# Closing MLP weights in units of two row tiles by 512 columns

## The chip, the cores and the metric

The kernel runs on one core of a Trainium2 chip. The metric is the device time of one execution in microseconds, the median of several runs. TensorE is PE in the rows, its weight loads are PEld, VectorE is DVE, ScalarE is ACT, GpSimd is POOL and SyncE is SP, which issues the transfers.

## What is computed

A trunk of four layers over 640 tokens (128 context, 512 latent) of width 1024. Each layer has a mixer (differential attention, neighbourhood attention, grouped-query attention, Hyena) and a squared-ReLU MLP, each with modulation, a gate and a layer norm:

```
for i in range(DEPTH):                                   # 4 layers
    mod_p = split(silu_ctx @ ada_w[i] + ada_b[i], 6)     # mod_s likewise, from c
    hp, hs = modulate(xp, mod_p[0], mod_p[1]), modulate(xs, mod_s[0], mod_s[1])
    op, os_ = mixer_i(hp, hs)
    xp = layer_norm(DN_ALPHA * xp + mod_p[2] * op, ...)  # xs likewise
    fp = relu(modulate(xp, mod_p[3], mod_p[4]) @ mlp_w1[i]) ** 2 @ mlp_w2[i]   # 1024 -> 4096 -> 1024
    xp = layer_norm(DN_ALPHA * xp + mod_p[5] * fp, ...)  # xs likewise
```

## The kernel before

All 640 tokens go through the weights together, as five tiles of 128 (`NT`). Values are fp32; for a matmul each operand is split into a rounded part and a rest, and `mm3` (lines 471 to 475) issues three matmuls: weights high with data high, weights high with data low, weights low with data high. Each matmul has its own weight load.

Weights come in units of 128 by 1024 fp32 (512 KB) in a fixed order that `weight_order` lists. `wget` (line 461) hands out a unit, starts transfers three ahead and splits units two ahead: a cast on ACT (line 450) and a difference on DVE (line 451, `hl`).

The MLP (`mlp`, line 865) runs in eight chunks of four row tiles of the hidden width. For chunk `ch` it first makes four opening units (`w1_unit`: 48 matmuls of 320 columns into a pair of banks, then Relu, Square and a split into `ff[ch]`), then it closes chunk `ch - 1` with four closing units (`w2`). A closing unit is four row tiles by 256 output columns. `quarter` (line 809) makes one group of 12 matmuls of 256 columns for each token tile, in which the `ff` tiles are the stationary operand and the weights move, and `residual` (line 647) evacuates it: a product with the gate on DVE (line 653, `gtmp`, three buffers) and an add into the residual `r` (line 660), three of four on POOL in layers 0 to 2 and all on DVE in layer 3. Chunk 7 is closed in `sublayer_end`, by `quarter` too.

Between the units, `side` (line 1530) does work of later layers, one slot behind each opening and each closing unit: a step of the next layer's modulation (`ada_step`, line 528: four multiply-adds on DVE of 128x512; at the last of eight steps, which falls behind a chunk's last closing unit, a sum over partitions by four matmuls with ones, and a copy), and, before the Hyena layer, filters (`hy_taps`, layer 0: two matmuls of 512 columns and the product `win`, line 1576; `tap_step` every third closing group) and their transforms (`hy_dft`, `hy_dft_ctx`, layers 1 and 2).

PSUM has eight banks: `b1` and `f1`, two single banks each, which `any1` (line 336) hands out in turn, and `b2` (line 340), a ring of two places of two banks each. Before the change the opening units and the filters take `b2`; closing groups, modulation sums (`ada`, `adat`) and the context transform (`hsc`) take `any1`.

The order of POOL's instructions is that of the program; those of PE, DVE and ACT are put in order when the kernel is built, by a planner with modelled durations, from the program's order as priority.

Of the kernel before, what the change touches and what calls it, by code (L numbers as in the profile page):

```python
# [18 lines left out]
P = 128  # L19
# [5 lines left out]
NT = TOK // P  # L25
# [4 lines left out]
DEPTH = 4  # L30
# [26 lines left out]
TSTEP = 3  # L57
# [138 lines left out]
def unit_b(w, k0, c0):  # L196
    return w[k0 * P:(k0 + 4) * P, c0:c0 + 256].reshape(4, P, 256).transpose(1, 0, 2).reshape(P, 1024)


def prepare(inp):  # L200
    g = {n: np.asarray(a) for n, a in inp.items()}
    o = lat_order()
    d = dict(shape_constants())
    x = np.concatenate([g["x_prompt"][0], g["x_sample"][0][o]], 0)
    d["x_tok"] = x.reshape(NT, P, D).transpose(1, 0, 2)
    d["x_t"] = x.T.reshape(KD, P, TOK).transpose(1, 0, 2)
    d["cvec"] = np.stack([g["c_ctx"], g["c"][0]], -1).reshape(KD, P, 2).transpose(1, 0, 2)
    d["ada_w"] = g["ada_w"]
    d["ada_b"] = g["ada_b"]
    d["ada_s"] = g["ada_w"][:, :, :2 * D].reshape(DEPTH, KD, P, 2, KD, P)[0].transpose(3, 1, 0, 2, 4).reshape(KD, P, 2 * D)  # L210
    d["ada_bt"] = g["ada_b"].reshape(DEPTH, 6, KD, P)[:, MODS].transpose(3, 0, 1, 2)
    d["ln_t"] = np.stack([g["ln_g"], g["ln_b"]], 2).reshape(DEPTH, 2, 2, KD, P).transpose(4, 0, 1, 2, 3)
    d["ln_g"] = g["ln_g"]
    d["ln_b"] = g["ln_b"]
    d["w1"] = np.stack([np.stack([unit_a(g["mlp_w1"][l], np.arange(f * P, f * P + P)) for f in range(32)]) for l in range(DEPTH)])
    d["w2"] = np.stack([np.stack([unit_b(g["mlp_w2"][l], 4 * ch, q * 256) for ch in range(8) for q in range(4)]) for l in range(DEPTH)])
    for nm, wq, cf in (("da", g["da_w_qkv"][0], da_cols), ("na", g["na_w_qkv"][0], na_cols)):
        d[nm + "_qk"] = np.stack([unit_a(wq, s * D + cf(j)) for j in range(8) for s in range(2)])
        d[nm + "_v"] = np.stack([unit_b(wq, 4 * kh, 2 * D + 256 * gr) for gr in range(4) for kh in range(2)])
    wq = g["gq_w_qkv"][0]  # L220
    d["gq_qk"] = np.stack([unit_a(wq, D + pair_cols(128 * i, 128 * i + 64)) for i in range(2)] + [unit_a(wq, gq_cols(j)) for j in range(8)])
    d["gq_v"] = np.stack([unit_b(wq, 4 * kh, 1280) for kh in range(2)])
    d["hy_in"] = np.stack([unit_a(g["hy_w_in"][0], np.arange(P) + p * D + (2 * gr + ct) * P) for gr, p in hy_parts() for ct in range(2)])
    rows = np.concatenate([np.arange(h * 64, h * 64 + 64) for j in range(8) for h in gq_heads(j)])
    for nm, wo in (("da", g["da_w_o"][0]), ("na", g["na_w_o"][0]), ("gq", g["gq_w_o"][0][rows]), ("hy", g["hy_w_o"][0])):
        d[nm + "_o"] = np.stack([unit_b(wo, 4 * kh, q * 256) for kh in range(2) for q in range(4)])
    ck = g["cache_da_k"][0, 0].reshape(P, D)
    d["da_ck"] = np.stack([ck[:, da_cols(j)].T for j in range(8)])
    ck = g["cache_na_k"][0, 0].reshape(P, D)
    d["na_ck"] = np.stack([ck[:, na_cols(j)].T for j in range(8)])  # L230
    ck = g["cache_gq_k"][0, 0].reshape(P, 256)
    d["gq_ck"] = np.stack([ck[:, pair_cols(128 * i, 128 * i + 64)].T for i in range(2)])
    for nm in ("da", "na", "gq"):
        d[nm + "_cv"] = g[f"cache_{nm}_v"].reshape(P, -1)
    d["da_lam"] = g["da_lambda"].reshape(1, 256)
    d["da_sub"] = g["da_subln_g"].reshape(P, 1)
    kc = np.arange(3 * P) // ROWS - 16
    rk = np.arange(3 * P) % ROWS
    qc, rq = np.arange(P) // ROWS, np.arange(P) % ROWS
    rr = rk[None, :] - rq[:, None] + 7  # L240
    cc = np.clip(kc[None, :] - qc[:, None], -15, 15) + 15
    d["na_bias"] = g["na_rel_bias"][0][:, rr, cc]
    both = pair_cols(0, 64) % 64
    part = both.reshape(2, 2, 32)[:, ::-1].reshape(-1)
    d["gq_g"] = np.stack([g["gq_q_norm"][0][both], g["gq_q_norm"][0][part], g["gq_k_norm"][0][both], g["gq_k_norm"][0][part]], 1)
    d["hy_sw"] = np.concatenate([g["hy_short_w"][0], g["hy_short_b"]], 0).reshape(4, 3, KD, P).transpose(3, 1, 2, 0)
    d["hy_w1"] = g["hy_ffn_w1"][0]
    d["hy_w2"] = g["hy_ffn_w2"][0]
    d["hy_b"] = np.stack([g["hy_ffn_b1"][0], g["hy_ffn_b2"][0], g["hy_ffn_freq"][0]], 1)
    w3 = g["hy_ffn_w3"][0].reshape(64, 2, 2, 4, 256).transpose(1, 3, 0, 2, 4).reshape(2, 4, 64, 512)  # L250
    ld = g["hy_log_decay"].reshape(2, 2, 4, 256).transpose(0, 2, 1, 3).reshape(2, 4, 1, 512)
    d["hy_w3"] = np.concatenate([np.concatenate([w3, w3], 2), np.broadcast_to(ld, (2, 4, P, 512))], 3)
    d["hy_fb"] = g["hy_filter_bias"][0]
    return {n: np.ascontiguousarray(a) for n, a in d.items()}
# [24 lines left out]
class Trunk:  # L279
# [248 lines left out]
    def ada_step(self, raw, l, m, k):  # L528

        nc = self.nc  # L530
        if k == 0:
            self.tn += 1
            self.acc = self.scr.tile([P, 2, D], F32, tag="ada", bufs=1, name=f"ada{self.tn}")
        acc = self.acc
        for h in range(2):
            for s in range(2):
                x, y = self.sil[:, k, s:s + 1], acc[:, s, h * 512:(h + 1) * 512]
                if k == 0:
                    nc.scalar.activation(y, raw[h], AF.Copy, scale=x)
                else:  # L540
                    nc.vector.scalar_tensor_tensor(out=y, in0=raw[h], scalar=x, in1=y, op0=ALU.mult, op1=ALU.add)  # L541
        if k < KD - 1:
            return
        ps = self.any1([P, 512], "ada")
        for g in range(4):
            nc.tensor.matmul(ps[32 * g:32 * g + 32], self.ones, acc[:, g // 2, g % 2 * 512:g % 2 * 512 + 512], start=True, stop=True)
        row = self.S(F32, "adarow", 512)
        if m in MODS:
            nc.scalar.copy(row, ps)
            pt = self.any1([P, 4, P], "adat")  # L550
            for j in range(4):
                nc.tensor.transpose(pt[:, j], row[:, j * P:(j + 1) * P], self.ident)
            mod = self.modt[l % 2][:, MODS.index(m)].rearrange("p (h j) s -> p h j s", j=4)
            bias = self.adab[:, l, MODS.index(m)].rearrange("p (h j) -> p h j", j=4)
            for s in range(2):
                src = pt[:, :, 64 * s:64 * s + 64:32].rearrange("p j h -> p h j")
                nc.vector.tensor_add(mod[:, :, :, s], src, bias)
            return
        bias = self.S(F32, "adabias", 512)
        nc.gpsimd.memset(bias, 0.0)  # L560
        for g in range(4):
            c = m * D + g % 2 * 512
            nc.sync.dma_start(bias[32 * g:32 * g + 1], self.a["ada_b"][l:l + 1, c:c + 512])
        nc.vector.tensor_add(row, ps, bias)
        for g in range(4):
            c = g % 2 * 512
            nc.sync.dma_start(self.gate_d[l, GATES.index(m), g // 2:g // 2 + 1, c:c + 512], row[32 * g:32 * g + 1])
# [297 lines left out]
    def mlp(self, l, nxt, last):  # L865
        nc = self.nc
        self.share = QL if last else QM
        ff = {}
        groups = 0
# [21 lines left out]
        def w1_first():  # L891
# [15 lines left out]
                        evac([ff[0][:, n, 2 * pair:2 * pair + 2, c0:c1] for n in range(2)], ps[:, :, :c1 - c0])  # L907
            self.settle()

        for ch in range(8):  # L910
            ff[ch] = self.L(F32R, f"ff{ch}").rearrange("p (a f t) -> p a f t", a=2, f=4)
            if ch == 0:
                w1_first()
                self.load_gates(l, 1)
                continue
            if ch == 6:
                self.load_ln(l, 1, last)
            for f in range(4):
                w1_unit(4 * ch + f)
                self.side()  # L920
            for q in range(4):
                u = self.wget(("w2", l, 4 * (ch - 1) + q))
                for t in range(NT):
                    self.quarter(u, ff[ch - 1], t, q)
                    groups += 1
                    if self.taps and groups % TSTEP == 0:
                        self.tap_step()
                self.side()
        while self.taps:
            self.tap_step()  # L930
        self.sublayer_end(l, 1, lambda q, ahead: self.wget(("w2", l, 28 + q), ahead), lambda u, t, q, quick: self.quarter(u, ff[7], t, q, quick), last, nxt in (1, 3), nxt in (1, 2))
# [678 lines left out]
    def hy_dft_ctx(self, i, x):  # L1610
        nc = self.nc
        tab = self.tab[2]
        for n in range(2):
            ps = self.any1([P, 512], "hsc")
            for s in range(2):
                c = slice(n * 512 + s * 256, n * 512 + s * 256 + 256)
                f = slice(s * P, s * P + P)
# [3 lines left out]
            o, g = divmod(2 * i + n, 4)  # L1621
# [599 lines left out]
```

## Time and profile before

| | us |
|---|---|
| median of 3 runs | 3448.93 (3448.27 to 3449.49) |
| profiled execution | 3451.18 |
| span of the profiled execution, first to last instruction | 3449.3 |
| PE busy | 3303.5 (96%) |
| DVE busy | 2573.7 (75%) |
| ACT busy | 1513.0 (44%) |
| POOL busy | 961.5 (28%) |

Times in rows are microseconds from the span's start. A matmul's row gives its start and its duration from operand to result; matmuls overlap, so the distance between two starts is what a matmul takes of PE's time.

### The profile page before, as it was taken

The page shows a single profiled execution, that of the slowest core. Times are in us where ns is not written, and L with a number is a line of the kernel's source. Part 1 is how long each engine was busy: PE and PEld are TensorE (multiplying, and loading weights), DVE is VectorE, ACT ScalarE, POOL GpSimd, SP SyncE. Part 2 cuts the span into 40 slices and gives each one's busy share as a digit, 9 for nine tenths or more (in the row PEclk, how much of TensorE's full clock was granted, in tenths as well). Part 3 has the DMA queues.
Part 4 walks back from the last instruction along what each step waited for, and adds up shares of the span by engine and source line. Part 5 has one row for each costly group of instructions (what it writes and reads, how often), then busy time and mean ns, then how long its engine had stood idle before and what let it go on. Part 6 is the DMA issues. An engine that isn't in the chain of part 4 may idle for free.

```text
span 3449.3 us, 63752 instructions
## 1 busy us (share of the span) xinstructions
PE 3303.5 (96%) x25288; PEld 3172.8 (92%) x25288; DVE 2573.7 (75%) x4806; ACT 1513.0 (44%) x2704; POOL 961.5 (28%) x912
## 2 busy tenths in 40 slices
PE   8999899999999999999998999999998999999998
PEld 6878899999999899999997889999998998999998
DVE  4777888788586678777677888887759888845457
ACT  3555453333366654333345665333425334432322
POOL 0333233334254433122242014232323112500002
PEclk9999999999999999999999999999999999999999
DMA  7343134545242325555412112545433224322221
GB/s 273 124 133 109 58 125 165 172 161 180 91 131 77 102 74 172 183 168 201 141 66 70 31 54 92 190 154 183 161 105 118 82 79 156 112 76 74 88 78 50
DMA packets 157643, 418.96 MB, mean 121 GB/s; under 512 B 19550, under 2 KB 29414, under 8 KB 154270
## 3 DMA queue, kind: packets, MB, share of 16 engines
q1 hardware_dynamic: 157344, 414.88, 36.3%
q8 instruction: 199, 3.26, 0.4%
q14 instruction: 100, 0.82, 0.1%
HBM read 371.20 MB, written 34.05 MB: 117 GB/s over the span
## 4 chain that ended last, share of the span: by engine, by line
PE 53%; DVE 14%; issue 5%; DMA 3%; ACT 2%; POOL 1%; SPq 0%; DVEq 0%; POOLq 0%; ACTq 0%
PE w L473 12%; PE w L474 12%; PE w L475 12%; DVE hl L451 2%; DVE ada L541 2%; DMA adaw<-in_ada_w 2%; PE pv L2048 2%; DVE gtmp L653 2%; PE s L2001 1%; PE ptp L1051 1%; PE qk L473 1%; PE qk L475 1%; PE qk L474 1%; DVE r L660 1%; PE py L1764 1%
## 5 line engine op out<-in xcount | busy, mean ns | idle before, releaser
L451 DVE TENSOR_TENSOR hl<-raw,hl 128x1024 fp32r<-128x1024 f32 x411 | 540.4, 1317 | 322.7 <-ACT hl L450 321.4
L450 ACT CAST hl<-raw 128x1024 fp32r<-128x1024 f32 x411 | 430.6, 1049 | 687.0 <-PE w L475 539.3
L660 POOL TENSOR_TENSOR r<-r,gtmp 128x256 f32<-128x256 f32 x416 | 413.4, 1007 | 1122.1 <-DVE gtmp L653 1073.3
L473 PE MATMUL w<-hl,ff 128*128 128x256 f32 x2560 | 716.6, 280 | 9.4 <-DVE gtmp L653 9.2
L474 PE MATMUL w<-hl,ff 128*128 128x256 f32 x2560 | 715.7, 280 | 2.5 <-DVE hl L451 2.5
L475 PE MATMUL w<-hl,ff 128*128 128x256 f32 x2560 | 714.3, 279 | 0.0
L473 PE MATMUL w<-hh,hl 128*128 128x320 f32 (+2 forms) x2048 | 635.4, 310 | 3.1 <-ACT fx L875 2.5
L474 PE MATMUL w<-hl,hl 128*128 128x320 f32 (+2 forms) x2048 | 631.8, 309 | 3.4 <-DVE hl L742 3.4
L475 PE MATMUL w<-hh,hl 128*128 128x320 f32 (+2 forms) x2048 | 631.9, 309 | 0.0
L473 PEld LDWEIGHTS w<-hl,ff 128*128 128x128 f32 x2560 | 481.5, 188 | 14.7 <-DVE gtmp L653 12.7
L474 PEld LDWEIGHTS w<-hl,ff 128*128 128x128 f32 x2560 | 481.7, 188 | 5.0 <-DVE hl L451 3.4
L475 PEld LDWEIGHTS w<-hl,ff 128*128 128x128 f32 x2560 | 480.4, 188 | 0.0
L653 DVE TENSOR_TENSOR gtmp<-w,gate 128x256 f32<-128x256 f32 x800 | 326.5, 416 | 179.1 <-PE w L475 165.1
L541 DVE SCALAR_TENSOR_TENSOR ada<-adaw,sil,ada 128x512 f32<-128x512 f32 x504 | 387.8, 801 | 91.9 <-DMA adaw<-in_ada_w 85.4
L473 PEld LDWEIGHTS w<-hh,hl 128*128 128x128 f32 x2048 | 384.1, 188 | 17.9 <-issue 8.4
L474 PEld LDWEIGHTS w<-hl,hl 128*128 128x128 f32 x2048 | 384.2, 188 | 4.1 <-DVE hl L742 4.1
L475 PEld LDWEIGHTS w<-hh,hl 128*128 128x128 f32 x2048 | 384.2, 188 | 0.8 <-issue 0.8
L875 ACT ACTIVATE fx<-w 128x640 f32<-128x640 f32 (+2 forms) x136 | 91.6, 674 | 461.2 <-PE w L475 447.8
L473 PE MATMUL qk<-hh,hl 128*128 128x320 f32 (+2 forms) x672 | 214.9, 320 | 0.5 <-ACT q L977 0.3
L474 PE MATMUL qk<-hl,hl 128*128 128x320 f32 (+2 forms) x672 | 210.6, 313 | 3.6 <-DVE hl L742 3.6
L475 PE MATMUL qk<-hh,hl 128*128 128x320 f32 (+2 forms) x672 | 210.6, 313 | 0.8 <-DVE hl L451 0.8
L473 PE MATMUL w<-hl,oh 128*128 128x256 f32 x640 | 184.3, 288 | 9.8 <-DVE gtmp L653 5.4
(342 smaller groups left out, 6970.7 us busy)
## 6 DMA issues: line engine op xcount, KB each, us to landing
raw<-in_w SPq DMA_DIRECT2D x256, 512.0 KB
adaw<-in_ada_w SPq DMA_DIRECT2D x288, 256.0 KB
adaw<-in_ada_w SPq DMA_DIRECT2D x16, 1024.0 KB
raw<-ab_d SPq DMA_DIRECT2D x32, 512.0 KB
raw<-in_hy_in SPq DMA_DIRECT2D x24, 512.0 KB
adaw<-in_ada_s SPq DMA_DIRECT2D x8, 1024.0 KB
raw<-in_da_qk SPq DMA_DIRECT2D x16, 512.0 KB
gate<-gate_d SPq DMA_DIRECT2D x32, 256.0 KB
```

Of the source, the lines that this page charges most:

```text
L450: self.nc.scalar.copy(t[:, 0], raw)
L451: self.nc.vector.tensor_sub(t[:, 1], raw, t[:, 0].bitcast(F32))
L473: mm(ps, w[0], x[0], start=start, stop=False)
L474: mm(ps, w[0], x[1], start=False, stop=False)
L475: mm(ps, w[1], x[0], start=False, stop=stop)
L541: nc.vector.scalar_tensor_tensor(out=y, in0=raw[h], scalar=x, in1=y, op0=ALU.mult, op1=ALU.add)
L653: nc.vector.tensor_mul(tmp, ps, self.gate[2 * s + q // 2][:, (q % 2) * 256:(q % 2) * 256 + 256])
L660: eng.tensor_add(rv, rv, tmp)
L875: nc.scalar.activation(x, src, AF.Relu)
L1051: nc.tensor.transpose(ps[:, i * P:(i + 1) * P], pr[:, (done + i) * P:(done + i + 1) * P], self.ident)
L1764: mm(py[ct][:, par], yh[:, i, cc], inv[h][:, kt, s, par], start=kt == 0 and i == 0 and h == 0, stop=False)
L2048: nc.tensor.matmul(ps[64 * h:64 * h + 64], self.v[:, self.chunk + c, vc:vc + 64], pts[h][:, c * P:(c + 1) * P], start=c == 0, stop=c == se ...
```

## The change

The closing weights of chunks 0 to 6 are laid out in units of two row tiles by 512 columns. A half of the output (512 columns) takes two such units: the first opens a bank of 512 columns for each of the five token tiles, six matmuls of 512 columns each; the second adds six more to each and closes it, and two residuals of 256 columns follow. Four of the five banks come from `any1`, the fifth is one half of a `b2` tile (`two`) that is held over both halves of a chunk. Because these five stay open, the modulation sum and its transposes take one `b2` tile (`both`) instead of two from `any1`, and `hsc` takes a `b2` tile. Chunk 7 keeps its units of four row tiles by 256 columns.

```diff
+def unit_w(w, k0, c0):
+    return w[k0 * P:(k0 + 2) * P, c0:c0 + 512].reshape(2, P, 512).transpose(1, 0, 2).reshape(P, 1024)
+
+def close_units(w, ch):
+    if ch < 7:
+        return [unit_w(w, 4 * ch + 2 * kp, h * 512) for h in range(2) for kp in range(2)]
+    return [unit_b(w, 4 * ch, q * 256) for q in range(4)]
...
-        ps = self.any1([P, 512], "ada")
+        both = self.b2([P, 2, 512], "ada")
+        ps = both[:, 0]
...
-            pt = self.any1([P, 4, P], "adat")
+            pt = both[:, 1].rearrange("p (a b) -> p a b", a=4)
...
+        def wide_part(u, ch, kp, t, ps):
+            c = slice(t * P, (t + 1) * P)
+            for k in range(2):
+                f = slice(k * 512, (k + 1) * 512)
+                self.mm3(ps, (ff[ch][:, 0, 2 * kp + k, c], ff[ch][:, 1, 2 * kp + k, c]), (u[:, 0, f], u[:, 1, f]), kp + k == 0, kp + k == 2)
...
-            for q in range(4):
-                u = self.wget(("w2", l, 4 * (ch - 1) + q))
-                for t in range(NT):
-                    self.quarter(u, ff[ch - 1], t, q)
-                    groups += 1
-                    if self.taps and groups % TSTEP == 0:
-                        self.tap_step()
-                self.side()
+            for h in range(2):
+                pss = [self.any1([P, 512], "w2") for _ in range(NT - 1)]
+                if h == 0:
+                    two = self.b2([P, 2, 512], "w2")
+                pss.append(two[:, h])
+                for kp in range(2):
+                    u = self.wget(("w2", l, 4 * (ch - 1) + 2 * h + kp))
+                    for t in range(NT):
+                        wide_part(u, ch - 1, kp, t, pss[t])
+                        if kp:
+                            for i in range(2):
+                                self.residual(pss[t][:, i * 256:i * 256 + 256], t, 2 * h + i)
+                        groups += 1
+                        if self.taps and groups % TSTEP == 0:
+                            self.tap_step()
+                    self.side()
...
-            ps = self.any1([P, 512], "hsc")
+            ps = self.b2([P, 2, 512], "hsc")[:, 0]
```

## Rows read from the trace of the kernel before

**Rows 1.** The page: busy us and shares; granted clock by slices; chain by line.
```profile
PE 3303.5 (96%) x25288; PEld 3172.8 (92%) x25288; DVE 2573.7 (75%) x4806; ACT 1513.0 (44%) x2704; POOL 961.5 (28%) x912
...
PEclk9999999999999999999999999999999999999999
...
PE w L473 12%; PE w L474 12%; PE w L475 12%; DVE hl L451 2%; DVE ada L541 2%; DMA adaw<-in_ada_w 2%; PE pv L2048 2%; DVE gtmp L653 2%; PE s L2001 1%; PE ptp L1051 1%; PE qk L473 1%; PE qk L475 1%; PE qk L474 1%; DVE r L660 1%; PE py L1764 1%
```

**Rows 2.** Windows: from:to, length, busy PE PEld DVE ACT POOL, clock, DMA, GB/s.
```profile
700.10:766.70 66.60, 63.01 (x456) 59.30 (x456) 53.56 (x85) 25.24 (x36) 21.85 (x22) 1.00 0.53 174
3099.80:3156.20 56.40, 56.40 (x434) 56.40 (x433) 28.90 (x53) 16.25 (x20) 0.00 (x0) 1.00 0.24 76
```

**Rows 3.** Groups by line: shapes xcount | busy us, mean ns | idle before.
```profile
L653 DVE TENSOR_TENSOR gtmp<-w,gate 128x256 f32<-128x256 f32 x800 | 326.5, 416 | 179.1 <-PE w L475 165.1 <-POOL r L660 12.4
...
L660 DVE TENSOR_TENSOR r<-r,gtmp 128x256 f32<-128x256 f32 x364 | 166.0, 459 | 7.7
...
L660 POOL TENSOR_TENSOR r<-r,gtmp 128x256 f32<-128x256 f32 x416 | 413.4, 1007 | 1122.1 <-DVE gtmp L653 1073.3 <-DVE m L2006 27.6 <-DVE mv L691 15.2
...
L451 DVE TENSOR_TENSOR hl<-raw,hl 128x1024 fp32r<-128x1024 f32 x411 | 540.4, 1317 | 322.7 <-ACT hl L450 321.4
...
L541 DVE SCALAR_TENSOR_TENSOR ada<-adaw,sil,ada 128x512 f32<-128x512 f32 x504 | 387.8, 801 | 91.9 <-DMA adaw<-in_ada_w 85.4 <-ACT ln_b L795 5.4 <-ACT ada L539 1.1
```

**Rows 4.** Timeline, PE, layer 0, closing: start us, us, engine, line, out<-in, shapes.
```profile
700.64 0.40 PE L1572 MATMUL filt<-hl,hab 128*128 128x512 f32 x1
...
701.12 0.28 PE L473 MATMUL w<-hl,ff 128*128 128x256 f32 x1
...
705.36 0.40 PE L1572 MATMUL filt<-hl,hab 128*128 128x512 f32 x1
...
705.82 0.28 PE L473 MATMUL w<-hl,ff 128*128 128x256 f32 x1
...
709.90 0.40 PE L1572 MATMUL filt<-hl,hab 128*128 128x512 f32 x1
```

**Rows 5.** Timeline, PE, layer 3: starts of closing, opening and next closing phase.
```profile
3039.64 0.28 PE L473 MATMUL w<-hl,ff 128*128 128x256 f32 x1
...
3067.91 0.31 PE L473 MATMUL w<-hh,hl 128*128 128x320 f32 x1
...
3096.07 0.28 PE L473 MATMUL w<-hl,ff 128*128 128x256 f32 x1
```

**Rows 6.** Waits of weight loads (us, times, longest): layer 0 twice, 1, 2.
```profile
PEld ada L546 <- DVE ada L541: 13.7, 11, 2.3
...
PEld w L473 <- DVE gtmp L653: 5.3, 4, 1.7
...
PEld w L473 <- DVE gtmp L653: 1.5, 3, 0.8
...
PEld w L473 <- DVE gtmp L653: 6.7, 10, 1.2
```

**Rows 7.** Timeline, ACT and PE, layer 1, around `hsc`.
```profile
1514.47 0.58 ACT L1620 COPY hout<-hsc 128x512 f32<-128x512 f32 x1
...
1513.52 0.32 PE L473 MATMUL w<-hh,hl 128*128 128x320 f32 x1
```

**Rows 8.** Timeline, PE and DVE, layer 1, end of a closing phase.
```profile
1503.04 0.28 PE L475 MATMUL w<-hl,ff 128*128 128x256 f32 x1
...
1503.84 0.74 DVE L653 TENSOR_TENSOR gtmp<-w,gate 128x256 f32<-128x256 f32 x2
...
1503.25 1.77 PE L546 MATMUL ada<-ada,ones 128*32 128x512 f32 x8
1504.94 0.41 PE L473 MATMUL w<-hh,hl 128*128 128x320 f32 x1
```

**Rows 9.** Timeline, DVE, layer 0: product of the filter starting at 700.64.
```profile
701.81 0.67 DVE L1576 TENSOR_TENSOR win<-win,filt 128x512 f32<-128x512 f32 x1
```

More of the change, by code (lines that the diff above doesn't have):

```diff
@@ L215, in prepare @@
     d["w1"] = np.stack([np.stack([unit_a(g["mlp_w1"][l], np.arange(f * P, f * P + P)) for f in range(32)]) for l in range(DEPTH)])
-    d["w2"] = np.stack([np.stack([unit_b(g["mlp_w2"][l], 4 * ch, q * 256) for ch in range(8) for q in range(4)]) for l in range(DEPTH)])
+    d["w2"] = np.stack([np.stack([u for ch in range(8) for u in close_units(g["mlp_w2"][l], ch)]) for l in range(DEPTH)])
     for nm, wq, cf in (("da", g["da_w_qkv"][0], da_cols), ("na", g["na_w_qkv"][0], na_cols)):
```

## Prediction

> **What bounds the kernel now.** I read the page first. TensorE is busy 96% of the span and its granted clock stands at the upper level, 2.4 GHz, in every slice; the chain that ended last runs for 36% of the span over the three lines of `mm3` alone [rows 1]. So the span is set by how closely matmuls follow each other and by the moments in which they don't. Then the windows by MLP chunk, for what stands beside PE: in layer 3 a chunk takes 56.4 us with PE never idle and DVE busy for 29 us; a chunk of layer 0 takes 66.6 us, PE misses 3.6 us of it and DVE is busy for 54 us, since the next layer's modulation and the filters are made between the units [rows 2]. There DVE is the second bound. Per closing unit of five groups (7.07 us of PE, a quarter of rows 5) it has 5 products of 416 ns, 1.25 adds of 459 ns, one weight split of 1317 ns and four modulation steps of 801 ns, 7.2 us in all [rows 3], and it falls behind whenever filters come on top.
>
> **What the change does on PE.** In 4 layers x 7 chunks, 240 matmuls of 256 columns become 120 of 512: 3360 pairs become single matmuls over the same columns, with 3360 weight loads fewer. What a matmul costs is the distance between starts, not the duration of a row, since they overlap. A run of 36 starts takes 4.24 us (701.12 to 705.36, 117.8 ns each), another one 4.08 us (705.82 to 709.90, 113.3 ns) [rows 4]; a closing phase of layer 3 takes 28.27 us for 240, 117.8 again, and the opening phase behind it 28.16 us for 192 of 320 columns, 146.7 ns [rows 5]. The slow spacing is the commoner; I put a pair at 234 ns, an estimate between 235.6 and 226.7. For 512 columns the nearest rows are the filter matmuls: two take 0.48 us in one place and 0.46 in another, so 230 to 240 ns each [rows 4]. The step from 256 to 320 columns says (146.7 - 117.8) / 64 = 0.45 ns per column, so 117.8 + 256 x 0.45 = 233 at 512. I take 231, as the filters that are followed by the fast spacing do. **Gain 3 ns x 3360 = 10 us.** Bounds: 240 loses 20 us; two fast spacings, 226.7, gain 25 us.
>
> The Trainium skill (TensorE: Matmul & The Clock Gate, section Back-to-back issue gap) gives the isolated distance as the columns over 2.4 GHz plus about 2.5 ns, 216 ns at 512 columns. By that a pair would gain 18 ns, and the sum below would come to 3390 us. The rows speak against it already at 256 columns, where the rule gives 109 ns and the trace 113 to 118 [rows 4].
>
> **What it does to the evacuations.** Products and adds stay as many (20 and 20 per chunk), but no group closes in the first unit of a half, and each of the five closes with two residuals in the second. A bank is taken again four groups later, 5.6 us, instead of three, 4.2 us. Load of a second unit in layers 0 to 2: 10 x 0.416 + 2.5 x 0.459 + 1.3 + 3.2 = 9.8 us in 7.07; of a first: 4.5. So DVE ends a half up to 2.7 us later than with the even load; the longer reach of a bank (1.4 us) and the quiet unit behind it cover that. In layer 3 all adds are on DVE: 10 x (0.416 + 0.459) + 1.3 = 10 us in 7.07 [rows 3]; 3 us behind at the end, covered by the 5.6. POOL has 7.5 adds of 1.007 us in a burst, 7.6 us against 7.07, which three `gtmp` buffers take up. What goes: the waits of PE's weight loads for `gtmp`, 5.3 us in layer 0, 1.5 in layer 1 and 6.7 in layer 2 [rows 6]. **Gain 13.5 us**; bounds 0 (they only move to the end of the phase) and 13.5. Next to be late is then the modulation sum behind DVE's queue, for which PE waits 13.7 us in layer 0 today [rows 6]; I leave that as it is.
>
> **What it does to the two-bank ring.** `b2` has two places. One is now held by `two` for a whole closing phase, and the modulation sums and `hsc` move into the same ring, from banks where they met nobody. Three prices:
> - `hsc`, four times in layer 1, between two opening units. The next opening unit then needs the place of its first part, whose copy ends at 1515.05; today that unit starts at 1513.52 [rows 7]. **Loss 4 x 1.5 = 6 us**; bounds 0 (the copy placed ahead of the other ACT work) and 6.
> - the modulation sum, which falls on the end of a chunk's closing phase 6 times in each of layers 0 to 2, 18 in all. It takes the free place, so the next opening unit needs `two`, and with it the last tile's residual. Today the last product ends at 1504.58, 1.5 us behind the start of the last closing matmul (1503.04), and the opening unit starts at 1504.94, behind the sum [rows 8]: no wait, 0.4 us to spare. With the burst the last tile comes 1.4 to 2.7 us later: 1.0 to 2.3 us of wait. Nothing is paid if the planner puts the opening unit ahead of the sum, in the free place. I take 0.4 us, nearer to today's rows. **Loss 18 x 0.4 = 7 us**; bounds 0 and 41.
> - the filters of layer 0, 40 of them, in one place instead of two: a filter needs the product `win` of the one before. They start 4.7 us apart [rows 4], and that product ends at 702.48, 1.84 us behind its filter's start [rows 9]. **Loss 2 us**; bounds 0 and 10 (in the bursts a quarter of them waits 1 us).
>
> Transfers are as many, as large and in the same order, and no instruction of SP or POOL is moved past another one's wait.
>
> **The sum.** The profiled execution took 3451.2 us, a span of 3449.3 and 1.9 around it, 2.3 above the median of the runs, 3448.9; I take the differences from the profile and set them against the median: -10 - 13.5 + 6 + 7 + 2 = -8.5 us, so 3440 us.
>
> **The rivals.**
> 1. *The ring takes it back (slower).* The place: the first opening unit of a chunk in layers 0 to 2, waiting for `two`. The other terms leave a gain of 15.5 us, so it decides from 15.5 / 18 = 0.9 us per chunk. At 1.9 us, the middle of what the burst makes, it costs 34 us: 3467. For it: DVE's queue is full in these phases; the sum already waits for it in layer 0 [rows 6]. Against it: in layer 0 that wait stands in the same spot and would cover it.
> 2. *Nothing to be seen.* In layers 0 to 2 DVE sets the pace of the phase, PE's 3 ns turn into waits for it, and the `gtmp` waits come back at its end. Then layer 3 alone gains, 7 x 120 x (235.6 - 231) = 3.9 us, less the 6 us of `hsc`: 3451; with half of the waits gone 3444. For it: the DVE share of layer 0 [rows 2].
> 3. *The weight loads were the bound.* PEld is busy 92% [rows 1]. If a load holds each start at 256 columns and hides behind 512, the columns pass at the granted 2.4 GHz, 213 ns: 21 x 3360 = 70 us, some 3380. Against it: rows 4, and the rise of 0.45 ns per column, which a bound by loads would not show. The rule of the Trainium skill named above would come out here.
>
> **How the numbers follow.** Forecast 37%, 3440 (3428 to 3442); rival 2 27%, 3442 to 3456; rival 1 31%, 3456 to 3490; rival 3 5%. About 0.2% (7 us) is what a measurement of this kernel can tell from no change. Faster by more: 37 + 5 = 42%; within: 27%; slower: 31%. The range takes the forecast with the stream's bound of 25 us, all of rival 2 and most of rival 1: 3418 to 3476, leaving out rival 3 and the tail of rival 1, some 15%.
>
> **What would show it.** Step 1: in layer 3 a closing phase goes from 28.27 to 27.7 us, 120 starts 231 ns apart; 27.2 would be the gaining bound, 28.8 the losing one, 25.6 rival 3. Step 2: no waits of weight loads for `gtmp` inside the closing phases. Step 3: waits of opening units for the copy of `hsc` in layer 1; waits of the first opening unit for `gtmp`, or of filters for `win`, in layers 0 to 2. The prediction is wrong if a closing phase of layer 3 doesn't move, or if the planner, which orders PE, DVE and ACT anew, opens gaps in stages that the change does not touch.

## The result, and the profile after

The changed kernel takes **3506.11 us** (median of 4 runs, 3501.96 to 3510.02) against 3449.21 for the kernel before (4 runs, 3448.27 to 3459.46): a ratio of **1.0153** with a 95% interval of 1.0141 to 1.0166, slower by some 57 us where 9 us of gain were forecast. The profiled execution took 3505.66 us with a span of 3503.9, so spans are compared below: 3503.9 - 3449.3 = 54.6 us.

First the page of the changed kernel: busy us and share of each engine.

```profile
PE 3311.5 (95%) x21928; PEld 3027.5 (86%) x21928; DVE 2543.4 (73%) x4806; ACT 1512.5 (43%) x2704; POOL 904.4 (26%) x912
```

The 3360 matmuls and as many weight loads are gone (25288 to 21928, [rows 1]), and yet PE is busy 8 us longer. The totals can't say why; the windows of the four closing stages do. A stage here runs from the first matmul of the closing phase of chunk 0 to that of chunk 6, six chunks in all; layers 0 to 3, first before, then after (columns as in [rows 2]).

```profile
500.65:892.40 391.75, 378.67 (x2736) 358.28 (x2735) 309.90 (x507) 146.38 (x202) 138.81 (x132) 0.99 0.49 161
1341.22:1722.30 381.08, 377.64 (x2886) 369.65 (x2885) 289.49 (x428) 142.85 (x183) 99.70 (x92) 1.00 0.52 174
2166.28:2542.49 376.21, 371.52 (x2851) 363.29 (x2849) 285.04 (x425) 136.50 (x173) 105.66 (x92) 1.00 0.51 168
3039.64:3378.20 338.56, 338.56 (x2594) 338.56 (x2593) 173.59 (x312) 97.49 (x120) 0.00 (x0) 1.00 0.25 79
```

```profile
501.87:928.53 426.66, 387.13 (x2017) 328.36 (x2015) 306.07 (x507) 146.66 (x202) 127.26 (x132) 0.95 0.45 148
1377.91:1769.28 391.37, 380.14 (x2169) 338.61 (x2168) 281.73 (x426) 142.62 (x183) 79.25 (x92) 0.99 0.52 169
2215.13:2600.67 385.54, 372.05 (x2134) 334.19 (x2133) 281.92 (x423) 136.45 (x173) 81.69 (x92) 0.99 0.49 163
3100.02:3433.78 333.76, 333.76 (x1875) 304.18 (x1873) 157.56 (x312) 97.45 (x120) 0.00 (x0) 1.00 0.26 79
```

Layer 0 loses 34.9 us, layer 1 loses 10.3, layer 2 loses 9.3, layer 3 gains 4.8. What lies behind layer 3's stage gains 1.0 more, and what lies ahead of and between the stages, with a closing phase of chunk 6 in each gap, loses 6 together, which isn't followed up here: 54.6 us in all. Length less PE's busy time, the time in which PE does nothing, goes from 13 to 40 us in layer 0, from 3 to 11 in layer 1 and from 5 to 13 in layer 2. The granted clock falls too, above all in layer 0 (0.99 to 0.95).

**Where PE waits in layers 0 and 2 after the change** (matmul by line, what released it: us in total, times, longest; layer 0, then layer 2):

```profile
PE filt L1599 <- DVE win L1603: 13.4, 9, 4.0
PE ada L558 <- DVE win L1603: 12.8, 4, 5.4
PE ada L558 <- DVE gtmp L665: 5.7, 2, 4.0
PE w L484 <- DVE gtmp L665: 4.2, 2, 2.1
...
PE w L484 <- DVE gtmp L665: 9.4, 5, 4.7
PE hs L484 <- DVE gtmp L665: 4.1, 2, 2.5
```

Nearly all of these are users of the two-bank ring: filters waiting for the filter before, sums waiting for a filter or for the held tile, opening units (`w`) and transforms (`hs`) waiting for the held tile. Only one `w` wait, of 0.3 us in layer 2, is a closing group that waits for a bank. The `gtmp` of the others is the last residual of a chunk, behind which `two` comes free.

### The profile page after: what moved, and what is told of

It reads as the page before. It is cut to its first block, busy times and chain, and to the rows that moved or that the text cites. A ratio compares the mean times of both kernels' runs of the same rounds, so it can differ in the third digit from the quotient of the medians.

```text
span 3503.9 us, 56911 instructions
## 1 busy us (share of the span) xinstructions
PE 3311.5 (95%) x21928; PEld 3027.5 (86%) x21928; DVE 2543.4 (73%) x4806; ACT 1512.5 (43%) x2704; POOL 904.4 (26%) x912
## 4 chain that ended last, share of the span: by engine, by line
PE 67%; DVE 17%; issue 5%; POOL 4%; ACT 4%; DMA 3%; SPq 0%; DVEq 0%; POOLq 0%; ACTq 0%
PE w L484 15%; PE w L486 15%; PE w L485 15%; DVE hl L462 2%; PE qk L484 2%; POOL r L672 2%; PE qk L486 2%; PE qk L485 2%; PE s L2028 2%; DVE gtmp L665 2%; DMA adaw<-in_ada_w 2%; PE ptp L1078 2%; PE pv L2075 2%; DVE r L672 1%; DVE ada L552 1%
## 5 line engine op out<-in xcount | busy, mean ns | idle before, releaser
L462 DVE TENSOR_TENSOR hl<-raw,hl 128x1024 fp32r<-128x1024 f32 x411 | 532.0, 1297 | 495.7 <-ACT hl L461 494.8
L672 POOL TENSOR_TENSOR r<-r,gtmp 128x256 f32<-128x256 f32 x416 | 348.3, 861 | 999.7 <-DVE gtmp L665 966.7
L485 PE MATMUL w<-hl,ff 128*128 128x512 f32 (+1 forms) x1440 | 529.4, 368 | 0.5 <-DVE hl L462 0.5
L486 PE MATMUL w<-hl,ff 128*128 128x512 f32 (+1 forms) x1440 | 529.8, 368 | 0.0
L484 PE MATMUL w<-hl,ff 128*128 128x512 f32 (+1 forms) x1440 | 526.1, 366 | 0.6 <-DVE gtmp L665 0.6
L552 DVE SCALAR_TENSOR_TENSOR ada<-adaw,sil,ada 128x512 f32<-128x512 f32 x504 | 364.9, 770 | 98.8 <-DMA adaw<-in_ada_w 88.9
L484 PEld LDWEIGHTS w<-hh,hl 128*128 128x128 f32 x2048 | 389.3, 190 | 47.7 <-issue 27.7
L486 PEld LDWEIGHTS w<-hh,hl 128*128 128x128 f32 x2048 | 389.0, 190 | 2.5 <-issue 2.5
L665 DVE TENSOR_TENSOR gtmp<-w,gate 128x256 f32<-128x256 f32 x800 | 311.2, 416 | 57.1 <-PE w L486 27.6
L484 PEld LDWEIGHTS w<-hl,ff 128*128 128x128 f32 x1440 | 270.4, 188 | 49.2 <-ACT hl L461 2.0
L485 PEld LDWEIGHTS w<-hl,ff 128*128 128x128 f32 x1440 | 270.7, 188 | 47.5 <-DVE hl L462 0.8
L486 PEld LDWEIGHTS w<-hl,ff 128*128 128x128 f32 x1440 | 270.9, 188 | 43.9
```

Source lines behind the costliest of these rows:

```text
L462: self.nc.vector.tensor_sub(t[:, 1], raw, t[:, 0].bitcast(F32))
L484: mm(ps, w[0], x[0], start=start, stop=False)
L485: mm(ps, w[0], x[1], start=False, stop=False)
L486: mm(ps, w[1], x[0], start=False, stop=stop)
L665: nc.vector.tensor_mul(tmp, ps, self.gate[2 * s + q // 2][:, (q % 2) * 256:(q % 2) * 256 + 256])
L672: eng.tensor_add(rv, rv, tmp)
```

## One such wait, followed through the engines

Layer 2 of the changed kernel, end of a closing phase: timeline of PE, then of DVE, then of POOL (start us, us, engine, line, out<-in, shapes, and in brackets the idle time before and what ended it).

```profile
2370.65 0.40 PE L486 MATMUL w<-hl,ff 128*128 128x512 f32 x1
2370.98 1.27 PE L558 MATMUL ada<-ada,ones 128*32 128x512 f32 x8
2377.00 0.39 PE L484 MATMUL w<-hh,hl 128*128 128x320 f32 x1 [4.75 <-DVE gtmp L665]
2377.23 0.31 PE L485 MATMUL w<-hl,hl 128*128 128x320 f32 x1
2377.38 0.34 PE L486 MATMUL w<-hh,hl 128*128 128x320 f32 x1
2377.52 0.47 PE L484 MATMUL w<-hh,hl 128*128 128x320 f32 x1
2377.79 0.47 PE L485 MATMUL w<-hl,hl 128*128 128x320 f32 x1
```

```profile
2367.30 2.08 DVE L552 SCALAR_TENSOR_TENSOR ada<-adaw,sil,ada 128x512 f32<-128x512 f32 x3 [5.39 <-DMA adaw<-in_ada_w]
2369.30 0.75 DVE L665 TENSOR_TENSOR gtmp<-w,gate 128x256 f32<-128x256 f32 x2
...
2371.41 1.07 DVE L665 TENSOR_TENSOR gtmp<-w,gate 128x256 f32<-128x256 f32 x3
...
2373.00 1.39 DVE L462 TENSOR_TENSOR hl<-raw,hl 128x1024 fp32r<-128x1024 f32 x1
...
2376.43 0.42 DVE L665 TENSOR_TENSOR gtmp<-w,gate 128x256 f32<-128x256 f32 x1 [0.17 <-POOL r L672]
```

```profile
2371.90 3.07 POOL L672 TENSOR_TENSOR r<-r,gtmp 128x256 f32<-128x256 f32 x3 [1.30 <-DVE gtmp L665]
2375.67 3.08 POOL L672 TENSOR_TENSOR r<-r,gtmp 128x256 f32<-128x256 f32 x3 [0.70 <-DVE gtmp L665]
```

DVE works in order. It stands 5.39 us for the transfer of a modulation weight, with the products of the burst queued behind that step. Then products alternate with adds (DVE's own and POOL's, 1.0 us each, through three `gtmp` buffers), and a weight split of 1.39 us lies among them. The last product ends at 2376.85, 6.2 us after the last closing matmul started; before, in the like place of layer 1, it was 1.5 us [rows 8]. The modulation sum has taken the ring's free place at 2370.98, so the first opening unit needs `two` and starts at 2377.00.

This end of a phase is the latest of its kind. Over the twelve ends in the stages of layers 1 and 2, the last product ends 0.7 to 2.1 us after the start of the last closing matmul before the change, and 1.8 to 6.2 us after it. In layer 0 it was 2.8 to 6.9 us before already, and is 4.0 to 11.6 us after.

And when PE goes on, it soon does so at half speed: from 2377.52 on the starts stand 0.27 us apart instead of 0.15. The granted clock of the stretch (columns as in [rows 2]) is 0.50, the lower level of 1.2 GHz:

```profile
2377.50:2380.90 3.40, 3.40 (x15) 3.40 (x14) 1.53 (x2) 0.00 (x0) 1.71 (x2) 0.50 0.03 7
```

## The experiments

The theory after this reading: the ring took it back, by three users (the sums, `hsc`, the filters) that meet the held tile. Rivals: the held tile alone is dear, whoever else uses the ring; or the burst of residuals is what costs, and the ring only shows it. A stage's length differs between kernels that don't touch it by 2 to 3 us (391.1 and 394.1 in layer 0 of e4 and e5, where 391.8 stood before); a difference below that is not read. The stage table below is from the windows of the traces, us for six chunks. Each time is set beside the median of the kernel before in the same round of runs, which is why that figure differs a little from run to run.

| | layer 0 | layer 1 | layer 2 | layer 3 |
|---|---|---|---|---|
| before | 391.8 | 381.1 | 376.2 | 338.6 |
| after | 426.7 | 391.4 | 385.5 | 333.8 |
| e1: before, sums and `hsc` in the ring | 410.6 | 383.7 | 374.1 | 338.6 |
| e2: before, one bank of five in a held tile | 404.6 | 380.4 | 369.4 | 338.6 |
| e3: after, sums and `hsc` back on `any1` | 416.9 | 374.2 | 366.2 | 333.8 |
| e4: e3's form in layer 3 alone | 391.1 | 379.7 | 373.6 | 333.8 |
| e5: e3's form in layers 1 to 3 | 394.1 | 374.6 | 366.2 | 333.8 |
| e6: e3, every second filter in the idle half of `two` | 405.4 | 374.3 | 366.6 | 333.8 |
| e7: after, only the sums back | 417.2 | 380.9 | 365.9 | 333.8 |
| e8: after, sums moved behind an opening unit | 416.4 | 383.6 | 368.7 | 333.8 |
| e9: before, no adds in layer 0 | 369.2 | 380.9 | 374.1 | 338.6 |
| e10: e6, no adds in layer 0 | 379.0 | 374.5 | 365.9 | 333.8 |
| e11: e6, half of layer 0's residuals put off | 398.8 | 374.4 | 366.9 | 333.8 |

**e1: only the ring's new users, on the kernel before.**

```diff
-        ps = self.any1([P, 512], "ada")
+        both = self.b2([P, 2, 512], "ada")
+        ps = both[:, 0]
...
-            pt = self.any1([P, 4, P], "adat")
+            pt = both[:, 1].rearrange("p (a b) -> p a b", a=4)
...
-            ps = self.any1([P, 512], "hsc")
+            ps = self.b2([P, 2, 512], "hsc")[:, 0]
```

> The kernel before, with only the modulation sums, their transposes and the context transform moved into the two-place ring b2; closing units stay four row tiles by 256 columns, and no place of the ring is held over a closing phase. If moving these into the ring is what costs (rival 1 in its plain form), some 10 to 20 us slower than before: 18 sums by up to 1 us and four transforms by 1.5 us. If the cost lies in the held place or in the residuals that come in bursts, within 6 us of before.

Measured: 3475.07 us against 3452.0, ratio 1.0070 (1.0055 to 1.0085), a little more than the 10 to 20 us expected, and not spread over 18 sums: of the loss, 18.8 us lie in layer 0, where the sums and the filters share two places (its PE waits in that stage):

```profile
PE w L473 <- DVE win L1577: 10.0, 3, 3.9
PE ada L547 <- DVE win L1577: 8.2, 3, 2.8
```

Layers 1 and 2 hardly move (+2.6 and -2.1). So where there are no filters, the sums in the ring cost next to nothing as long as nobody holds a place of it.

**e2: only the held place, on the kernel before.** The closing units stay narrow; the fifth token tile's groups go into halves of a held `two`.

```diff
+            two = self.b2([P, 2, 512], "w2")
             for q in range(4):
...
-                    self.quarter(u, ff[ch - 1], t, q)
+                    self.quarter(u, ff[ch - 1], t, q, False, two[:, q % 2, 0:256] if t == NT - 1 else None)
```

> The kernel before, with only the fifth token tile's closing groups put into a b2 tile that is held over the whole closing phase; units, residuals and the place of sums and transforms as before. If the held place is the cause (filters in one place instead of two, transforms too), 25 to 40 us slower than before, nearly all in layer 0, with PE waiting for the filter's product there. If the bursts of residuals are the cause, within 6 us of before.

Measured: 3460.23 against 3452.0, ratio 1.0026 (1.0016 to 1.0035): a loss of 8 us, between the two that were expected. Layer 0 loses 12.8 us, by filters that wait for the filter before, as one place is left to them; layer 2 gains 6.8, since a fifth bank helps the narrow groups as well: none of them waits for `gtmp` there any more. Waits of PE in layer 0:

```profile
PE filt L1574 <- DVE win L1578: 17.2, 9, 3.2
```

Neither half of the change to the ring costs anything in layers 1 and 2 by itself; there e1 and e2 add up to a gain of 7 us. What is lost there comes from both at once, with the burst; both without the burst weren't run.

**e3: the whole change, but sums and `hsc` on `any1` as before.**

```diff
-        both = self.b2([P, 2, 512], "ada")
-        ps = both[:, 0]
+        ps = self.any1([P, 512], "ada")
...
-            pt = both[:, 1].rearrange("p (a b) -> p a b", a=4)
+            pt = self.any1([P, 4, P], "adat")
...
-            ps = self.b2([P, 2, 512], "hsc")[:, 0]
+            ps = self.any1([P, 512], "hsc")
```

> The changed kernel with the modulation sums, their transposes and the context transform put back into the single banks. If their place in the ring is what costs, layers 1 and 2 lose the 22 us that they cost in the changed kernel and the whole comes to some 3480 us; layer 0 keeps most of its 36 us, since filters still have one place. If the bursts alone cost, no change: 3500 to 3508.

Measured: 3458.4 against 3452.0, ratio 1.0021 (1.0009 to 1.0034), some 22 us better than expected. Layers 1 and 2 are now faster than before, by 6.9 and 10.0 us, and in layer 2 PE never stands still (length and PE's busy time are equal):

```profile
2187.21:2553.42 366.21, 366.21 (x2130) 329.61 (x2129) 281.56 (x424) 136.33 (x173) 81.93 (x92) 1.00 0.52 172
```

The end of a phase that was followed above has its like here, with the same burst and the same stand of DVE for a modulation weight (5.34 us). The last product comes as late, and PE goes on behind the sum, in the free place (PE, then DVE):

```profile
2340.52 0.40 PE L486 MATMUL w<-hl,ff 128*128 128x512 f32 x1
...
2342.02 0.41 PE L484 MATMUL w<-hh,hl 128*128 128x320 f32 x1
```

```profile
2346.32 0.42 DVE L664 TENSOR_TENSOR gtmp<-w,gate 128x256 f32<-128x256 f32 x1 [0.19 <-POOL r L671]
```

So in these layers the burst needs nothing beyond what covers it; the loss was the ring. In layer 0 it is 25 us of the 34.9 that stay.

**e4 and e5: e3's form in some layers only.** A switch chooses, per layer, the wide loop or the one of before, and the weights are laid out to match; e5 has `WIDE = (1, 2, 3)`.

```diff
+WIDE = (3,)
...
+            if l in WIDE:
+                for h in range(2):
...
+            else:
+                for q in range(4):
```

> The change in layer 3 alone, where no side work uses the ring; layers 0 to 2 and the place of sums and transforms as before. If the stream gains what the trace of the changed kernel shows there (28.27 to 27.47 us per closing phase, seven of them), 3443 to 3444 us, 5.6 us under before. If a part of it is lost at the layer's end or start, 3446 to 3449.

> The change in layers 1 to 3, layer 0 as before, modulation sums and context transform in the single banks. In the run that put these back in all layers, layers 1, 2 and 3 came out 8, 10 and 5 us under before and layer 0 some 25 us over. If the filters of layer 0 are all that is left of the loss, this run is 20 to 24 us under before, some 3425 to 3430 us. If layers 1 and 2 gained only because layer 0 had left DVE less to do, it is no better than the run with layer 3 alone, 3443 to 3447.

Measured: e4 3446.52 against 3452.0, ratio 0.9984 (0.9975 to 0.9994); e5 **3434.58** against 3450.32, ratio **0.9955** (0.9940 to 0.9970). Layer 3 gains its 4.8 us and what lies behind it 1.0; layers 1 and 2 add 6.5 and 10.0. e4 lies in the worse of the two bands expected (3446 to 3449), e5 between its two. e5 beats both kernels, with the lowest time of all forms that keep the adds: wide closing units are worth having in every layer without filters.

**e7: the change with only the sums taken back**, `hsc` still in the ring (the first two hunks of e3).

> The changed kernel with only the modulation sums and their transposes put back into the single banks; the context transform of layer 1 stays in the ring. If the sums are what costs (rival 1), nearly all of the 47 us between the changed kernel and the run with both put back returns: 3460 to 3468 us, and layer 1 is 4 to 6 us over that run (four transforms by 1.0 to 1.5 us). If the transforms carry more than that, layer 1 stays 10 us or more over it.

Measured: 3466.67 against 3450.32, ratio 1.0047 (1.0032 to 1.0062). Against the changed kernel this gives the sums' price: 9.5 us in layer 0, 10.5 in layer 1, 19.6 in layer 2, 39.6 in all or **2.2 us for each of the 18**. The lower clock behind the waits is in this price. Against e3, e7 gives the price of `hsc`: 380.9 - 374.2 = 6.7 us in layer 1, where the wait is seen on PE as

```profile
PE w L484 <- ACT hout L1646: 2.6, 1, 2.6
```

and on its weight loads as 3.5 us in three waits. Only one of the three transforms in the stage makes PE stand still: behind the other two the planner has put a closing phase, not an opening unit. The chunk with the wait takes 70.0 us, from one closing phase to the next, where e3 takes 65.2.

**e8: the sums stay in the ring, but come later.** The step that ends a modulation row moves from behind the last closing unit to behind the first opening unit of the next chunk, which then finds the free place.

```diff
+            late = []
...
-                            out += ada[:1] + side[i // 4].get(4 * (ch - 1) + i % 4, [])
+                            out += late + (ada[:1] if i < 7 else []) + side[i // 4].get(4 * (ch - 1) + i % 4, [])
+                            late = ada[:1] if i == 7 else []
```

> The changed kernel, sums and transform still in the ring, with the last step of each modulation row and its sum moved behind the first opening unit of the next chunk, so that this unit finds the free place of the ring and the sum takes the place of `two`. From the first to the last closing phase layers 0, 1 and 2 take 426.7, 391.4 and 385.5 us in the changed kernel, and 417, 381 and 366 with the sums in the single banks. If the price of the sums is the opening unit that waits for `two` and its last residual, layers 1 and 2 drop to some 383 and 371 us (a place is still missing for part of an opening unit). If it is any meeting in a ring of two places, they stay at 388 to 391 and 382 to 386.

Measured: 3470.43 (two runs) against 3450.15, ratio 1.0057 (1.0037 to 1.0077). Layers 1 and 2 come to 383.6 and 368.7: of the sums' 30.1 us there, 24.6 go. In layer 2 no wait of an opening unit for `two` is left to speak of:

```profile
PE w L486 <- ACT fx L889: 1.4, 1, 1.4
PE w L486 <- ACT od L1633: 0.6, 1, 0.6
PE w L486 <- DVE gtmp L667: 0.3, 1, 0.3
```

The move also takes a row's last steps on DVE out of the burst, but that isn't what helps: where no transform falls on the end of a phase, the opening unit starts some 0.23 us after the last closing matmul, ahead of the last product (1.8 to 3.9 us after it). With e3 and e7 that settles what the sums' price in these layers is made of: not their banks as such, but the opening unit that finds the free place taken and must wait for the chunk's last residual. The same move saves 10.3 us in layer 0.

**e6: two places for the filters again.** On e3, every second filter goes into that half of `two` which is idle in the running half of the chunk.

```diff
+                self.spare = two[:, 1 - h]
...
-            ps = self.b2([P, 2, 512], "filt")[:, 0]
+            self.flip = not self.flip
+            ps = self.spare if self.spare is not None and self.flip else self.b2([P, 2, 512], "filt")[:, 0]
```

> The changed kernel with modulation sums and context transform in the single banks, and every second filter of layer 0 put into the half of `two` that is idle in that half, so that filters have two places again while the closing tiles still hold one. If the one place left for the filters is what costs layer 0 its 25 us, layer 0 comes within 8 us of before and the whole to some 3430 to 3440 us. If the residuals in bursts (POOL and DVE) cost it, layer 0 stays 20 to 28 us over, 3450 to 3458 in all.

Measured: 3447.1 against 3450.32, ratio 0.9989 (0.9979 to 0.9999). Layer 0 gains **11.5 us** (416.9 to 405.4). It is still 13.6 us slower than before, between the 8 and the 20 that were expected, although its matmul stream is shorter. Its largest waits now are `w` behind a filter's product, filters in the spare half behind a residual (L1602 is that filter), and closing groups behind residuals:

```profile
PE w L485 <- DVE win L1606: 9.3, 6, 3.2
PE w L1602 <- DVE gtmp L665: 4.6, 4, 1.5
...
PE w L485 <- DVE gtmp L665: 2.7, 2, 1.6
```

Of the first row's 9.3 us, 7.5 (three waits, up to 3.2 us) are again opening units that wait for a place of the ring, which a filter holds until DVE has come to its product; the other 1.8 are closing groups.

**e9 and e10: is it the adds of the burst?** The kernel before and e6, each without the adds into `r` in the seven closing phases of layer 0.

```diff
         nc.vector.tensor_mul(tmp, ps, self.gate[2 * s + q // 2][:, (q % 2) * 256:(q % 2) * 256 + 256])
+        if self.leave:
+            return
```

> The kernel before with the adds into the residual left out in the closing phases of layer 0 (so the output is that of other numbers): the products stay. It is the level for the next run: layer 0 takes 391.8 us in the kernel before; without adds DVE has 5 adds of 0.46 us less per chunk and POOL none, so some 380 to 388 us.

> The run with two places for the filters (layer 0: 405.4 us, 13.6 over before), with the same adds left out. If the bursts cost through the adds (POOL's queue, in which they stand among the filters' differences, and the three gtmp buffers behind it), layer 0 comes to or under the level of the run before with the adds left out. If they cost through the products that come ten at a time on DVE, or through the shared place, it stays 8 to 14 us over that level.

Measured, a single run of each, beside 3450.15 for the kernel before: 3426.98 (e9) and 3418.28 (e10). Layer 0 of e9 takes 369.2 us, less than the 380 to 388 expected, and that of e10 379.0, a difference of 9.8 where it was 13.6 with the adds. By that number alone the adds would explain only 4 us. But the windows of the sum's line by itself in this stage (length, PE's and its weight loads' busy time in that line) show what the 9.8 are; e9, e10, then with adds the kernel before and e6:

```profile
501.60:870.80 369.20, 6.69 (x48) 1.08 (x48) 1.00 0.51 171
```

```profile
502.40:881.40 379.00, 16.02 (x48) 2.25 (x48) 1.00 0.51 166
```

```profile
500.65:892.40 391.75, 16.66 (x48) 2.38 (x48) 0.99 0.49 161
```

```profile
503.15:908.57 405.42, 16.88 (x48) 2.38 (x48) 0.99 0.48 155
```

In e9 alone the planner kept the eight records of each sum together (six blocks for six sums; the others have 12 blocks before, 13 in e6 and 15 in e10, at the places where parts of the row's last step on DVE come ready), and a part of a sum costs about as much as all of it:

```profile
659.10 1.06 PE L547 MATMUL ada<-ada,ones 128*32 128x512 f32 x8
```

```profile
658.70 1.05 PE L559 MATMUL ada<-ada,ones 128*32 128x512 f32 x2
663.02 1.05 PE L559 MATMUL ada<-ada,ones 128*32 128x512 f32 x4
665.51 1.05 PE L559 MATMUL ada<-ada,ones 128*32 128x512 f32 x2
```

(e9, then e10.) Outside that line the stage takes 375.1 us before and 388.5 in e6, 13.4 apart; without adds 362.5 and 363.0, 0.5 apart. Read so, the adds in the burst carry nearly all of the excess; read by the stage's length, some 4 us of it. The first reading takes the line's busy time as time of the path, and the second takes e9's undivided sums as if e10 could have had them; no run parted the two, so the share of the adds stays open between 4 and 13 us. Counted by starts, from a part of a sum to the next instruction of PE, the sums take 6.3 us in e9 and 15.1 in e10, and PE stands still for only 3.2 and 5.3 us of these stages. So their time is time of PE's path, which speaks for the larger share.

**e11: the same work, but no burst.** On e6, the second residual of a tile in layer 0 is put off by two groups, and the last ones go behind the first opening unit of the next chunk.

```diff
+                                if l == 0 and i and not (h and t == NT - 1):
+                                    wait.append((groups + 2, res))
+                                else:
+                                    res()
+                        while wait and wait[0][0] <= groups:
+                            wait.pop(0)[1]()
```

> The run with two places for the filters, with the second residual of each token tile in layer 0 put off by two groups (the last ones behind the first opening unit), so that a burst is spread over seven groups instead of five. If the burst is what is left of the loss in layer 0, it goes from 405 to some 396 to 400 us and the whole from 3447 to some 3440. If not, layer 0 stays at 403 to 407.

Measured: 3438.04 against 3450.15, ratio 0.9961 (0.9947 to 0.9975). Layer 0 gains 6.6 us on e6, so half of the remainder is the burst as a burst, with no work left out. 7 us over the kernel before remain there. Two waits of 2.6 us in them are still opening units behind a filter's product, so the ring (first row); the rest isn't shown.

```profile
PE w L485 <- DVE win L1618: 5.6, 4, 2.6
PE w L485 <- DVE gtmp L665: 5.5, 6, 2.0
```

This form too beats both kernels; it is level with e5, which leaves layer 0 alone.

## Why the prediction was wrong

The forecast was 3440, with 3418 to 3476 as range; the time is 3506, 30 us above the range. The sign and the mechanism were rival 1's, at more than its price. The lower end doesn't follow as it was worked out: 25 us for the stream in place of 10 gives 3425, not 3418. That changed nothing here.

| term | put at, us | measured, us |
|---|---|---|
| stream of 512 columns | -10 | 0.8 per closing phase: -4.8 in layer 3, about as much in layers 1 and 2, and -1.0 behind; not to be read in layer 0 |
| `gtmp` waits | -5.3 in layer 0, -1.5 and -6.7 in layers 1 and 2 | -2 and -5 of idle time in layers 1 and 2; not to be read in layer 0 |
| `hsc` | +6 | +6.7 |
| modulation sums in the ring | +7 | +39.6 |
| filters in one place | +2 | +11.5 |
| burst of residuals | 0 | 6.6 to 13.6 in layer 0, and none seen in layers 1 and 2 |

- **The stream was right, and the gain larger than taken.** Layer 3, starts of a closing phase, of the opening phase behind it and of the next closing phase, to be read against [rows 5]:

```profile
3100.02 0.39 PE L484 MATMUL w<-hl,ff 128*128 128x512 f32 x1
...
3127.48 0.31 PE L484 MATMUL w<-hh,hl 128*128 128x320 f32 x1
...
3155.64 0.39 PE L484 MATMUL w<-hl,ff 128*128 128x512 f32 x1
```

  The closing phase takes 27.46 us for 120, 228.9 ns each, where 27.7 was said and 28.27 stood; the opening phase keeps its 28.16. A slow pair gains 6.7 ns, inside the bounds given (240 to 226.7). Rival 3 falls with it: it needed 213. The weight loads' share fell from 92% to 86%, and no more than these 6.7 ns came of it. The Trainium skill (TensorE: Matmul & The Clock Gate, section Back-to-back issue gap) gives 216 ns at 512 columns for the isolated distance. This trace doesn't agree: it shows 228.9 in a stream of matmuls with a weight load each.
- **The `gtmp` waits went, with the banks that the sums had before.** e3 gains 6.9 and 10.0 us in layers 1 and 2; less the stream's 4.8 that is 2 and 5, against 1.5 and 6.7 in [rows 6]. The time in which PE stands still says the same: from 3.4 to 1.4 us and from 4.7 to none. In layer 2 nearly all of it was for `gtmp`; in layer 1 most of it (2.5 us) was for weight splits, so there the agreement is in part luck.
- **`hsc` came out at its price by luck**: 6.7 us against 6. The way was right for one transform, at 2.6 us of wait where 1.5 was said; the planner took two others out of it, and the rest lies in time in which PE is busy longer.
- **The modulation sum is the step that failed.** The place, the order of events and the bounds (0 to 41 us) were right; the choice in them was not. I took 0.4 us "nearer to today's rows", from one end of a closing phase in layer 1 where DVE was on time [rows 8], though the burst's load gave 1.0 to 2.3. For layers 1 and 2 that end was typical; in layer 0 DVE was 2.8 to 6.9 us late before the change already, and the price used no such end. The measured mean is 2.2. And the wait followed above shows what neither of the two figures had in it: DVE in order, standing 5.39 us for a transfer with the evacuations behind it. With the sums on their own banks that stand costs PE nothing (e3); in the ring it costs 4.75 us. In [rows 3] there are 85 us of such idle time, and I priced none of it.
- **The filters failed likewise.** I set the mean spacing of filters (4.7 us) against a product that came promptly, 1.84 us behind its filter's start [rows 9]. In the changed kernel PE's order has a filter at 610.55 behind a product that DVE could not start before 609.81, as it stood 2.11 us for a modulation weight:

```profile
608.48 1.41 DVE L552 SCALAR_TENSOR_TENSOR ada<-adaw,sil,ada 128x512 f32<-128x512 f32 x2 [2.11 <-DMA adaw<-in_ada_w]
609.81 0.68 DVE L1603 TENSOR_TENSOR win<-win,filt 128x512 f32<-128x512 f32 x1
...
610.55 0.80 PE L1599 MATMUL filt<-hl,hab 128*128 128x512 f32 x1 [4.05 <-DVE win L1603]
```

  With one place PE has nothing to do in the meantime. 11.5 us came of it, at the upper bound of 10 within what a stage's length can tell.
- **The burst was covered in layers 1 and 2, as said, and not in layer 0**, where filters and modulation steps fill DVE (54 of 66.6 us, [rows 2]). The cover (5.6 us of reach and a quiet unit) was worked out from mean loads and then used for all three layers alike; layer 0 had no bound of its own in the sum. e11 shows at least 6.6 us of it; the 13.6 that e6 leaves hold waits for the ring as well.
- **"In layer 0 that wait stands in the same spot and would cover it"**, said against rival 1, is refuted: e7 and e8 both recover some 10 us there.

The chances: rival 1 had 31% and was priced at 1.9 us per chunk, 34 us in all, near the 39.6 measured. But it was made the only loss; filters and burst were left at 2 and 0 in the same case, though the same condition, a DVE that runs late, makes all three.

## What to carry to other kernels

A tile that is held in a ring of two makes it a ring of one: price every other user of that ring by the worst lateness of the engine that frees the place, not by its mean load, and look for what that engine, working in order, may stand for. When several costs hang on the same condition, put them into the same case. A gain on the bounding engine can be kept by using the new form only where the shared resource is quiet: with sums and `hsc` on their own banks, three of four layers gained 0.45% here and all four lost 0.2%.

## What the runs showed of the hardware

- A wait of PE costs more than its length. Behind the 4.75 us at 2377.00 the matmuls of 320 columns go on at 0.27 us for a stretch, against 0.147 [rows 5], at a granted clock of 0.50. The mean granted clock of the whole span falls from 0.991 to 0.982; with levels at 1 and one half that is an estimate of 62 and 126 us at the lower level. The slices of [rows 1] show a 9 throughout all the same, as each stands for some 86 us. In layer 0 PE is busy 8 us longer with 720 matmuls fewer.
- Matmuls follow each other at about 0.45 ns per column from 256 to 512 columns (117.8, 146.7 and 228.9 ns at 256, 320 and 512), with a weight load for each. Half as many loads for the same columns gained no more than 6.7 ns in 235.6.
- Sums by four matmuls with ones, each for 32 rows of the output, take 1.05 us together, and again 1.05 us for each part when they are issued in parts (1.0 us each from start to the next start): 6.69 or 16.02 us for the same 48 records in e9 and e10.
